# Hybrid GDN/Mamba2 trunk on one core: unit loads on GpSimd's queue, the nested heads' decayed k on VectorE

## Chip, cores and metric

The kernel runs on one core of a Trainium2 chip (TRN2). The metric is the device time of one execution in microseconds (us), and the time of a kernel is the median over its runs. The core's engines have separate instruction queues and work side by side, held together by semaphores: TensorE (PE) for matmuls and transposes into PSUM, VectorE (DVE), ScalarE (ACT), GpSimd (POOL), and SyncE (SP), whose queue here does little but issue DMAs. An engine works through its queue strictly in order, so an instruction that waits holds up all that stand behind it.

## Reference

The reference is one layer (DEPTH = 1) of a macaron trunk over x of 1024 tokens by 1024 channels, in float32: half a SwiGLU, a mixer, half a SwiGLU, a final norm.

```python
x += 1/2 * SwiGLU(RMSNorm(x))                       # D_FF = 2816
h = RMSNorm(x);  p = h @ W_in                       # one combined W_in
x += W_out @ [ GDN_heads(p) || Mamba2_SSD_heads(p) ]   # 8 heads of 128, 16 heads of 64
x += 1/2 * SwiGLU(RMSNorm(x));  out = RMSNorm(x)

def gated_delta_rule(q, k, v, g, beta):             # CHUNK = 64
    q = l2_normalize(q) * dk ** -0.5;  k = l2_normalize(k);  gc = cumsum(g) in a chunk
    a_low = strict_lower(beta * (k @ k.T) * decay)
    t_inv = inverse(eye + a_low)
    u = t_inv @ (v * beta);  w = t_inv @ (k * beta * exp(gc))
    qk = (q @ k.T) * decay;  q_dec = q * exp(gc)
    k_dec = k * exp(gc[-1] - gc)                    # the decayed copy of k
    for each chunk:
        v_new = u - w @ S;  o = q_dec @ S + qk @ v_new
        S = S * exp(g_tot) + k_dec.T @ v_new
```

## The kernel before

**Stages.** The feed-forward parts, the Mamba2 heads and the projection W_in run first and last; in the middle of the program (about 1120 to 1425 us) lie the projections of the last GDN heads, woven into the delta rule of the heads before them. The change touches this middle alone.

**Nested heads.** NESTED is 3 (L654). GDN heads 0 to 2 get their q, k, v and gate z by plain matmuls. Heads 3 to 7, the nested ones, get them by a scheme of seven products in place of eight (Strassen's): the weights of a pair of 128-column blocks have been combined earlier into seven units, each a high and a low part of 128x512 float32 (512 KB), and lie in scratch memory as `wu_scr`. `chunk()` (L1266 to L1290) makes one pair in the order 1, 6, 2, 5, 7, 3, 4; two chunks for each of five heads make 70 units. Each unit is `unit_prod` (L1255): twelve matmuls of 128x512 (L1261 high by high, L1262 high by low, L1263 low by high) into a `pj` bank of PSUM, which ACT copies (L1275, L1280) or DVE adds up (L1271) into `pre`, `zc` and the like. A unit lies in one of four slots of SBUF, tile `wunits`; when the matmuls of unit s have been written, `unit_load(s + 4)` (L1247, its DMA L1252) issues the load of the unit that takes its slot. So a load waits for the last matmul on its slot, and has three units' time until its own first matmul.

**One head of the delta rule.** The causal convolution of q, k and v is an ACT scaling (L1294) and three taps on DVE (L847), with a Silu on ACT (L1419 for v, L1418 for z). `k_part(h)` (L1338): eight PE transposes of k (L1347), four into each of two `mx` banks; for each of the eight blocks, `jd`, a Square on ACT whose accumulator is the token's sum of squares (L1351), and `kd`, the block times `wend`, the decayed copy of k (L1356 on ACT; for the last head, 7, L1353 on DVE). `decays(h)` (L1362) loads the decays (L1366), takes ACT Exps (L1367, L1370) and masks on GpSimd (an affine select, L971). Then kk and qk: L1445 and L1446 write into the `mx` banks, so the first of them waits until `jd` and `kd` have read the bank; DVE makes `u` and `dt` of them (L1449, L1452).

**The inverse.** `u`'s diagonal blocks are stored (L1461) and read back (`fu`, L1488), `fx` is cleared on GpSimd (L1492, L1494), and a solve of 31 steps runs on DVE (L1498, L1500). Its result goes through DMA (L1503, L1510, L1511) and a DVE transpose (L1512). Then PE and the others alternate: L1518/L1519 on PE, L1521 two copies on DVE, L1525 to L1527 on PE, a memset of `x64` on GpSimd (L1529), copies of ACT and DVE (L1530 to L1534), L1539 on PE, L1541 on ACT, L1544 on PE. ACT's L1470 squares q for the head. The recurrence over chunks (L1556 to L1578) uses `kd` at L1570.

**What sets the order.** A tile framework's scheduler puts the instructions of each engine in order, from the dependencies and its own costs. Where a helper's instructions stand in the queue is therefore read from the order, not from the source. Two more loads of 1024 KB on GpSimd's queue, `y` (L1235) and `x` (L1234), fetch the first operands of the output projection (`group_tile`, L1212, matmuls L123 to L125), which begins when the units end, at about 1424.6 us.

Of the kernel before, what the change touches and what calls it, by code (L numbers as in the profile page):

```python
# [11 lines left out]
F32 = mybir.dt.float32  # L12
# [17 lines left out]
GH = 8  # L30
# [14 lines left out]
def kernel(  # L45
# [6 lines left out]
    nc = tc.nc  # L52
    V, A, G, T = nc.vector, nc.scalar, nc.gpsimd, nc.tensor
# [9 lines left out]
    def psum(tag):  # L63
        return ps.tile([P, 512], F32, name="ps_" + tag, tag=tag, bufs=PS_BUFS[tag])
# [9 lines left out]
    wu_scr = [dram.tile([P, 7, 2, 512], F32, name=f"wu_scr{i}") for i in range(2 * (GH - 3))]  # L74
# [579 lines left out]
    NESTED, UP_CHUNKS = 3, 8  # L654
# [592 lines left out]
    def unit_load(s):  # L1247

        if s < 7 * len(wu_scr):
            c, i = divmod(s, 7)  # L1250
            u = slots[s % 4]
            nc.sync.dma_start(out=u.bitcast(F32), in_=wu_scr[c][:, i])  # L1252
            units.append((s, u))

    def unit_prod(bank, m, first):  # L1255

        s, u = units.pop(0)
        bh, bl = H_IN[m]
        for k in range(4):
            wh, wl = (u[:, i, k * P:(k + 1) * P] for i in range(2))  # L1260
            T.matmul(bank, lhsT=wh, rhs=bh[k], start=first and k == 0, stop=False, skip_group_check=True)  # L1261
            T.matmul(bank, lhsT=wh, rhs=bl[k], start=False, stop=False, skip_group_check=True)  # L1262
            T.matmul(bank, lhsT=wl, rhs=bh[k], start=False, stop=k == 3, skip_group_check=True)  # L1263
        unit_load(s + 4)
# [48 lines left out]
    def first_units():  # L1313

        for i in range(2):
            t = wp.tile([P, 2, 2, 512], F32R, name="wunits", tag="wst")
            slots.extend(t[:, j] for j in range(2))
        for s in range(4):
            unit_load(s)
# [15 lines left out]
    with ExitStack() as cg:  # L1335
        g1 = cg.enter_context(tc.tile_pool(name="gdn1", bufs=1, reuse_waits="tile"))
        g2 = cg.enter_context(tc.tile_pool(name="gdn2", bufs=2, reuse_waits="tile"))
        def k_part(h, kt):  # L1338

            tk = g2.tile([P, NB], F32, name="tk")  # L1340
            br2 = g2.tile([P, NB], F32, name="br2")
            kd = g1.tile([P, NB, P], F32, name="kd", bufs=2)
            for half in range(2):
                pt = psum("mx")
                for i in range(4):
                    b = half * 4 + i
                    T.transpose(pt[:, i * P:(i + 1) * P], kt[:, b * P:(b + 1) * P], ident)  # L1347
                for i in range(4):
                    b = half * 4 + i
                    jd = g1.tile([P, P], BF16, name="jd")  # L1350
                    A.activation(out=jd, in_=pt[:, i * P:(i + 1) * P], func=AF.Square, accum_out=tk[:, b:b + 1])  # L1351
                    if h == GH - 1:
                        V.tensor_scalar(out=kd[:, b], in0=pt[:, i * P:(i + 1) * P],  # L1353
                                        scalar1=wend[:, b, h:h + 1], scalar2=None, op0=ALU.mult)
                    else:
                        A.mul(out=kd[:, b], in_=pt[:, i * P:(i + 1) * P], mul=wend[:, b, h:h + 1])  # L1356
            V.tensor_scalar(out=tk, in0=tk, scalar1=EPS, scalar2=None, op0=ALU.add)
            V.reciprocal(out=br2, in_=tk)
            V.tensor_tensor(out=br2, in0=br2, in1=beta[:, :, h], op=ALU.mult)
            return tk, br2, kd  # L1360
# [12 lines left out]
        for h in range(GH):  # L1373
# [25 lines left out]
            else:  # L1399
# [12 lines left out]
                if h < GH - 1:  # L1412
                    tk, br2, kd = k_part(h, kt)
                with tc.issue_after(copy.ins):
                    A.activation(out=qt, in_=qt, func=AF.Silu)
                if h < GH - 1:
                    conv_from(pre, 16 + h, vt_)
                    A.activation(out=zc, in_=zc, func=AF.Silu)  # L1418
                    A.activation(out=vt_, in_=vt_, func=AF.Silu)  # L1419
                else:  # L1420
                    out_start()
                    for b in range(FIRST_TILES):
                        for dh in range(2):
                            tile_end = group_tile(0, b, dh, *ready0[0])
                    tk, br2, kd = k_part(h, kt)
                    qe, dt = decays(h)
                    conv_from(pre, 16 + h, vt_)
                    A.activation(out=zc, in_=zc, func=AF.Silu)
                    A.activation(out=vt_, in_=vt_, func=AF.Silu)
            (G if h == GH - 1 else nc.sync).dma_start(out=z_scr[h], in_=zc)  # L1430
            if h < NESTED:
                tk, br2, kd = k_part(h, kt)
# [5 lines left out]
            u = g2.tile([P, NB, P], F32, name="u")  # L1438
# [68 lines left out]
            x64, mt2 = lv2[0:64, 0], lv2[:, 1]  # L1507
# [18 lines left out]
                T.matmul(px[64:96, ls], lhsT=mt[96:128, b], rhs=xd[96:128, b], start=True, stop=True)  # L1526
                T.matmul(px[32:64, ls], lhsT=xd[32:64, b], rhs=mt[32:64, b], start=True, stop=True)  # L1527
            pxv = px[:, 0:256].rearrange("p (b l) -> p b l", b=NB)
            G.memset(x64[0:32, :, 32:64], 0.0)  # L1529
            A.copy(out=x64[0:32, :, 0:32], in_=xtr[0:32])  # L1530
            A.copy(out=x64[32:64, :, 32:64], in_=xtr[32:64])
            A.mul(out=x64[32:64, :, 0:32], in_=pxv[32:64], mul=-1.0)
# [227 lines left out]
```

## Time and profile before

| | before |
|---|---|
| median of 3 runs | 2300.2 us (2300.33, 2298.66, 2300.2) |
| the profiled execution, its own time | 2300.99 us |
| its span | 2299.3 us |
| granted TensorE clock, mean | 0.997 |
| PE busy | 2253.7 us (98%) |
| PEld (weight loads) busy | 1839.1 us (80%) |
| DVE busy | 1764.1 us (77%) |
| ACT busy | 1176.9 us (51%) |
| POOL busy | 53.1 us (2%) |

The span is the time from the first to the last instruction of one profiled execution; 1.7 us of its own time lie around it, and it is 0.8 us above the median. Times in the trace count from the start of the span. `PE a L1 <- DVE b L2: 2.7, 1, 2.7` says that PE stood still at line 1 for 2.7 us in all, once, 2.7 us the longest, until DVE's line 2 had ended. In a timeline, a bracket at the end of a row is the idle time ahead of the instruction and what ended it.

### The profile page before, as it was taken

How to read it: one execution, taken by the hardware profiler on the slowest of the kernel's cores; microseconds unless marked ns; L12 is line 12 of the kernel's file. 1: busy time of each engine (PE TensorE's matmuls, PEld its weight loads, DVE VectorE, ACT ScalarE, POOL GpSimd, SP SyncE). 2: the span in 40 equal slices, each digit the busy share in tenths (PEclk: the TensorE clock that was granted, in tenths of full speed). 3: DMA queues.
4: the chain of work that ended last, by engine and by line, in shares of the span. 5: the costliest groups of instructions: out<-in, count | busy, mean ns of one | idle time of the engine just before them, and what ended most of it. 6: DMA issues, size and time to landing. Idle time of an engine off the chain costs nothing. (4 is left out here: it accounts for less than half of the span.)

```text
span 2299.3 us, 32056 instructions
## 1 busy us (share of the span) xinstructions
PE 2253.7 (98%) x11630; PEld 1839.1 (80%) x11630; DVE 1764.1 (77%) x3253; ACT 1176.9 (51%) x2279; POOL 53.1 (2%) x115
## 2 busy tenths in 40 slices
PE   7999999999999999999999999999999999999998
PEld 5788888888878878888777887788878888888886
DVE  7998999768777887657577777778688776766787
ACT  7444444354367886875555556623543333334344
POOL 0000000000000110100000000000000000000000
PEclk9999999999999999999999999999999999999999
DMA  3466686496654433242555655436123332329446
GB/s 112 142 228 239 229 274 220 170 336 218 202 183 137 133 120 101 74 131 65 184 164 158 184 164 192 140 99 219 65 88 126 99 113 94 117 87 346 145 151 215
DMA packets 268242, 371.64 MB, mean 162 GB/s; under 512 B 61480, under 2 KB 168076, under 8 KB 266292
## 3 DMA queue, kind: packets, MB, share of 16 engines
q1 hardware_dynamic: 267268, 366.88, 49.0%
q0 software_dynamic: 816, 2.72, 0.3%
q8 instruction: 91, 1.49, 0.3%
q14 instruction: 67, 0.55, 0.1%
HBM read 256.68 MB, written 112.86 MB: 161 GB/s over the span
## 5 line engine op out<-in xcount | busy, mean ns | idle before, releaser
L336 PE MATMUL ps_pj<-bh,al 128*128 128x512 f32 x688 | 267.9, 389 | 0.0
L335 PE MATMUL ps_pj<-bl,ah 128*128 128x512 f32 x688 | 267.8, 389 | 0.0
L334 PE MATMUL ps_pj<-bh,ah 128*128 128x512 f32 x688 | 267.5, 390 | 0.0
L123 PE MATMUL ps_pj<-hhi,whi 128*128 128x512 f32 x512 | 203.3, 397 | 0.4 <-ACT gsb L902 0.4
L125 PE MATMUL ps_pj<-hhi,wlo 128*128 128x512 f32 x512 | 203.7, 398 | 0.0
L124 PE MATMUL ps_pj<-hlo,whi 128*128 128x512 f32 x512 | 202.6, 396 | 0.0
L336 PEld LDWEIGHTS ps_pj<-bh,al 128*128 128x128 f32 x688 | 129.1, 188 | 26.8
L335 PEld LDWEIGHTS ps_pj<-bl,ah 128*128 128x128 f32 x688 | 129.2, 188 | 26.7
L334 PEld LDWEIGHTS ps_pj<-bh,ah 128*128 128x128 f32 x688 | 128.9, 188 | 26.6
L317 DVE TENSOR_TENSOR as<-wst 128x512 f32<-128x512 f32 x220 | 144.8, 689 | 2.0 <-DMA wst<-in_ffn_w_up_dram 1.8
L242 DVE TENSOR_TENSOR al<-as,ah 128x512 fp32r<-128x512 f32 x220 | 141.2, 687 | 4.9 <-ACT ah L241 4.3
L241 ACT CAST hid<-hraw 128x1024 fp32r<-128x1024 f32 (+1 forms) x84 | 82.2, 980 | 119.1 <-PE ps_oo L565 48.7
L334 PE MATMUL ps_mx<-bh,ah 128*128 128x512 f32 x352 | 138.6, 396 | 3.8 <-ACT m L343 1.4
L241 ACT CAST ah<-as 128x512 fp32r<-128x512 f32 x220 | 125.6, 618 | 30.3 <-DVE as L317 30.3
L335 PE MATMUL ps_mx<-bl,ah 128*128 128x512 f32 x352 | 138.4, 393 | 0.4 <-DVE bl L242 0.4
L336 PE MATMUL ps_mx<-bh,al 128*128 128x512 f32 x352 | 137.7, 391 | 0.3 <-DVE al L242 0.3
L241 ACT CAST ah<-wst 128x512 fp32r<-128x512 f32 x88 | 54.5, 621 | 155.9 <-PE ps_oo L335 94.4
L242 DVE TENSOR_TENSOR hid<-hraw,hid 128x1024 fp32r<-128x1024 f32 (+1 forms) x84 | 95.2, 1133 | 22.8 <-ACT hid L241 22.5
L123 PEld LDWEIGHTS ps_pj<-hhi,whi 128*128 128x128 f32 x512 | 96.3, 188 | 19.8 <-ACT gsb L902 0.9
L124 PEld LDWEIGHTS ps_pj<-hlo,whi 128*128 128x128 f32 x512 | 96.3, 188 | 19.3 <-issue 0.8
L125 PEld LDWEIGHTS ps_pj<-hhi,wlo 128*128 128x128 f32 x512 | 96.2, 188 | 19.3 <-issue 0.5
L564 PE MATMUL ps_pj<-wd,hid 128*128 128x512 f32 x264 | 103.4, 392 | 1.3 <-DVE wd L242 1.2
(505 smaller groups left out, 5704.6 us busy)
## 6 DMA issues: line engine op xcount, KB each, us to landing
wu_scr<-wunit SPq DMA_DIRECT2D x140, 256.0 KB, 3.5
hraw<-hid_scr SPq DMA_DIRECT2D x70, 512.0 KB, 3.8
wunits<-wu_scr SPq DMA_DIRECT2D x70, 512.0 KB, 4.1
hid_scr<-hs SPq DMA_DIRECT2D x110, 256.0 KB, 3.2
wst<-in_ffn_w_down_dram SPq DMA_DIRECT2D x50, 512.0 KB, 5.0
wst<-in_ffn_w_gate_dram SPq DMA_DIRECT2D x22, 1024.0 KB, 5.5
wst<-in_ffn_w_up_dram SPq DMA_DIRECT2D x22, 1024.0 KB, 8.6
hid_scr<-sg SPq DMA_DIRECT2D x44, 256.0 KB, 2.0
```

Source lines behind the costliest of these rows:

```text
L123: T.matmul(o, lhsT=wh, rhs=mh, start=first, stop=False)
L124: T.matmul(o, lhsT=wh, rhs=ml, start=False, stop=False)
L125: return T.matmul(o, lhsT=wl, rhs=mh, start=False, stop=last)
L241: return (A.copy(out=hi, in_=src), V.tensor_tensor(out=lo, in0=src, in1=hi.bitcast(F32), op=ALU.subtract))
L242: V.tensor_tensor(out=lo, in0=src, in1=hi.bitcast(F32), op=ALU.subtract))
L317: V.tensor_tensor(out=t, in0=v[0], in1=v[1], op=v[2])
L334: T.matmul(bank, lhsT=wh[:, k], rhs=bh[:, k], start=a, stop=False, skip_group_check=True)
L335: T.matmul(bank, lhsT=wh[:, k], rhs=bl[:, k], start=False, stop=False, skip_group_check=True)
L336: T.matmul(bank, lhsT=wl[:, k], rhs=bh[:, k], start=False, stop=z, skip_group_check=True)
L564: T.matmul(bank, lhsT=hh, rhs=wl, start=False, stop=False, skip_group_check=True)
```

## The change

Three lines change.

```diff
     def unit_load(s):
         if s < 7 * len(wu_scr):
             c, i = divmod(s, 7)
             u = slots[s % 4]
-            nc.sync.dma_start(out=u.bitcast(F32), in_=wu_scr[c][:, i])
+            G.dma_start(out=u.bitcast(F32), in_=wu_scr[c][:, i])
             units.append((s, u))
...
                     A.activation(out=jd, in_=pt[:, i * P:(i + 1) * P], func=AF.Square, accum_out=tk[:, b:b + 1])
-                    if h == GH - 1:
+                    if h >= NESTED:
                         V.tensor_scalar(out=kd[:, b], in0=pt[:, i * P:(i + 1) * P],
                                         scalar1=wend[:, b, h:h + 1], scalar2=None, op0=ALU.mult)
                     else:
                         A.mul(out=kd[:, b], in_=pt[:, i * P:(i + 1) * P], mul=wend[:, b, h:h + 1])
...
-            G.memset(x64[0:32, :, 32:64], 0.0)
+            V.memset(x64[0:32, :, 32:64], 0.0)
```

All 70 unit loads go from SP's queue to GpSimd's; the 32 `kd` of heads 3 to 6 go from ACT (L1356) to DVE (L1353); the eight memsets at L1529 go from GpSimd to DVE. No arithmetic is added or left out. The scheduler then orders the queues anew. On GpSimd, the loads stand in the order of the units but for two pairs that are swapped (48/49 and 52/53), between the `fx` memsets and affine selects of the heads; each waits for PE (its slot is free). PE's matmuls are the same, and in the same order up to head 3's `k_part`.

**Head 4.** PE's queue before, from the last transposes of head 4's `kt` to the first L1445 (`ps_mx_11574` and `ps_mx_11591` are the two banks, `ps_mx_11621` the bank of the first kk, `wunits` the slots, `hhi`, `hlo` and `t4`, `t6` the activations' parts; `[waits X]` names whom a row waits for):

```order
L1347 MATMUL ps_mx_11591<-ident_185,kt_11357 128x128 x4
L1261 MATMUL ps_pj_12041<-hhi_5516,wunits_10080 128x512 [waits DMAHW0_49]
L1262 MATMUL ps_pj_12041<-hlo_5520,wunits_10080 128x512
L1263 MATMUL ps_pj_12041<-hhi_5516,wunits_10080 128x512
L1261 MATMUL ps_pj_12041<-hhi_5516,wunits_10080 128x512
L1262 MATMUL ps_pj_12041<-hlo_5520,wunits_10080 128x512
L1263 MATMUL ps_pj_12041<-hhi_5516,wunits_10080 128x512
L1261 MATMUL ps_pj_12041<-hhi_5517,wunits_10080 128x512
L1262 MATMUL ps_pj_12041<-hlo_5521,wunits_10080 128x512
L1263 MATMUL ps_pj_12041<-hhi_5517,wunits_10080 128x512
L1445 MATMUL ps_mx_11621<-kt_11357 128x128 [waits Activation_49]
L1446 MATMUL ps_mx_11621<-qt_11356,kt_11357 128x128
```

PE's queue now, at the same L1445; the rows are the last of 26 unit matmuls that stand behind the transposes:

```order
L1262 MATMUL ps_pj_12056<-t6_10088,wunits_10080 128x512
L1263 MATMUL ps_pj_12056<-t6_10086,wunits_10080 128x512
L1261 MATMUL ps_pj_12041<-hhi_5518,wunits_10081 128x512 [waits DMASW6_49,Activation_49]
L1262 MATMUL ps_pj_12041<-hlo_5522,wunits_10081 128x512
L1445 MATMUL ps_mx_11621<-kt_11357 128x128 [waits DVE_49]
L1446 MATMUL ps_mx_11621<-qt_11356,kt_11357 128x128
```

The first L1445 has moved back on PE from behind 9 unit matmuls to behind 26, and it waits for DVE where it waited for ACT. In head 3 it has moved from behind 8 to behind 24, in head 6 it stands behind 26.

DVE's queue now, at the same place (`kd_11573` is head 4's; L847 are taps of its v, L1498 and L1500 the last steps of head 3's solve):

```order
L1353 TENSOR_SCALAR kd_11573<-ps_mx_11574,wend_5931 128x128 [waits Activation_49]
L1500 TENSOR_TENSOR fx_11029<-fx_11029,ft_11030 128x7x5 [waits DVE_49]
L847 SCALAR_TENSOR_TENSOR vt__11358<-pre_10673,cols_195,vt__11358 128x1024
L1498 TENSOR_TENSOR ft_11030<-fx_11029,fu_11024 128x28 [waits DVE_49]
L1353 TENSOR_SCALAR kd_11573<-ps_mx_11574,wend_5931 128x128 [waits Activation_49]
L1500 TENSOR_TENSOR fx_11029<-fx_11029,ft_11030 128x7x4 [waits DVE_49]
L847 SCALAR_TENSOR_TENSOR vt__11358<-pre_10673,cols_195,vt__11358 128x1024
L1498 TENSOR_TENSOR ft_11030<-fx_11029,fu_11024 128x24 [waits DVE_49]
L1353 TENSOR_SCALAR kd_11573<-ps_mx_11574,wend_5931 128x128 [waits Activation_49]
L1500 TENSOR_TENSOR fx_11029<-fx_11029,ft_11030 128x8x3 [waits DVE_49]
```

Between this third `kd` and the fourth stand five more steps of the solve (L1498, L1500 and so on) and the memset L1529; the second bank's four `kd` follow with one L1271 between. Before, no `kd` stood there, and the three taps stood together behind the solve. On ACT each `jd` of a nested head but the first now waits for DVE, as in head 7 before, so that `jd` and `kd` take turns.

**Head 5.** PE's queue before, in the inverse of head 4 (`lv2_11785` and `u_11620` are its operands; L979 and L1479 belong to the same head):

```order
L1261 MATMUL ps_pj_12738<-t3_8497,wunits_10081 128x512
L979 MATMUL ps_mx_12357<-qsq_12355,ones_193 32x256 [waits PE_49,Activation_49]
L1539 MATMUL ps_sc_11845<-lv2_11785,u_11620 64x64 [waits Activation_49,Pool_49]
L1539 MATMUL ps_sc_11845<-lv2_11785,u_11620 64x64 x7
L979 MATMUL ps_mx_12357<-qsq_12355,ones_193 32x256 x3
L1479 MATMUL ps_mx_12369<-ident_185,vt__12040 128x128 x4
L1262 MATMUL ps_pj_12738<-t3_8499,wunits_10081 128x512
L1263 MATMUL ps_pj_12738<-t3_8497,wunits_10081 128x512
L1544 MATMUL ps_sc_11855<-u_11620,lv2_11785 64x64 [waits DMAHW0_49,DMAHW6_49,DVE_49,Activation_49]
```

PE's queue now, in the same inverse; 36 unit matmuls stand between head 5's transposes and the first L1518, and the first row is the last of L1525 to L1527:

```order
L1527 MATMUL ps_sc_11814<-lv_11784 32x32
L1539 MATMUL ps_sc_11845<-lv2_11785,u_11620 64x64 [waits Activation_49]
L1539 MATMUL ps_sc_11845<-lv2_11785,u_11620 64x64 x7
L1544 MATMUL ps_sc_11855<-u_11620,lv2_11785 64x64 [waits DMAHW1_49,DMAHW7_49,DVE_49,Activation_49]
L1544 MATMUL ps_sc_11855<-u_11620,lv2_11785 64x64 x7
L1445 MATMUL ps_mx_12303<-kt_12039 128x128 [waits DVE_49]
L1446 MATMUL ps_mx_12303<-qt_12038,kt_12039 128x128
```

L1518, L1525, L1539, L1544 and head 5's first L1445 now stand one behind the other on PE with no unit matmul between; before, unit matmuls stood between each two of them, and the L1445 long ahead of them.

ACT's queue now, at the same place (`jd` reads head 5's first bank):

```order
L1351 ACTIVATE jd_12267,tk_12253<-ps_mx_12256 128x128 [waits Activation_49]
L1532 ACTIVATE lv2_11785<-ps_sc_11814 32x8x32 [waits PE_49]
L1470 ACTIVATE qsq_12355<-qt_12038 128x1024 [waits DMAHW2_49]
L1534 ACTIVATE u_11620<-ps_sc_11814 32x8x32 [waits DVE_49]
L1541 COPY lv2_11785<-ps_sc_11845 64x512 [waits PE_49]
L1351 ACTIVATE jd_12270,tk_12253<-ps_mx_12256 128x128 [waits Activation_49]
```

The third and fourth `jd` of head 5 stand on both sides of the inverse's ACT steps; before, the eight pairs of `jd` and `kd` stood on ACT in one piece, ahead of head 5's Silus.

## Prediction

> **What bounds the kernel now.** I read the page first, for the engine that fills the span.
>
> ```profile
> PE 2253.7 (98%) x11630; PEld 1839.1 (80%) x11630; DVE 1764.1 (77%) x3253; ACT 1176.9 (51%) x2279; POOL 53.1 (2%) x115
> ```
>
> PE is busy for 2253.7 of 2299.3 us. No line of the diff adds or removes a matmul, so the change can only act through the times at which PE stands still. Next comes the view by stretches, for the part from the first unit product to the last (columns: us, then busy us and instructions of PE, PEld, DVE, ACT and POOL, the granted clock, DMA share, GB/s), and the waits of PE in it.
>
> ```profile
> 1121.00:1426.00 305.00, 296.64 (x2045) 235.69 (x2045) 212.56 (x678) 175.09 (x497) 13.53 (x36) 0.99 0.59 174
> ```
>
> ```profile
> PE ps_pj L1261 <- DVE pre L1271: 2.7, 1, 2.7
> PE ps_mx L1445 <- ACT kd L1356: 1.6, 1, 1.6
> PE ps_sc L1556 <- DVE sn L1575: 1.3, 1, 1.3
> PE ps_oo L1567 <- ACT vn L1563: 0.9, 2, 0.5
> PE ps_sc L1561 <- DVE rr L1558: 0.6, 1, 0.6
> PE ps_sc L1518 <- DVE lv L1512: 0.2, 1, 0.2
> ```
>
> PE is idle for 305.00 - 296.64 = 8.4 us in the middle of the program, and the waits explain 7.3 of them. Two things follow. A gain from this change can't be much above 7.3 us. And no wait ends with a unit load: no row names L1252 or DMA. DVE, at 212.56 of 305.00 us, is the busier of the helpers; ACT has 175.09.
>
> I then asked for the tile that changes engine, and for its surroundings in head 4, where the 1.6 us wait lies.
>
> ```profile
> L1356 ACT ACTIVATE kd<-ps_mx,wend x56: 349/392/477, 1009.2 to 1368.8; 128x128 f32<-128x128 f32 x56
> L1353 DVE TENSOR_SCALAR kd<-ps_mx,wend x8: 318/350/351, 1438.5 to 1451.0; 128x128 f32<-128x128 f32 x8
> ```
>
> ```profile
> 1246.41 0.25 ACT L1351 ACTIVATE jd<-ps_mx 128x128 bf16<-128x128 f32 x1
> 1246.91 0.26 ACT L1351 ACTIVATE jd<-ps_mx 128x128 bf16<-128x128 f32 x1
> ...
> 1248.15 0.38 ACT L1356 ACTIVATE kd<-ps_mx,wend 128x128 f32<-128x128 f32 x1
> ```
>
> ```profile
> 1243.83 1.04 PE L1347 MATMUL ps_mx<-ident,kt 128*128 128x128 f32 x8
> 1244.63 0.47 PE L1261 MATMUL ps_pj<-hhi,wunits 128*128 128x512 f32 x1
> ...
> 1246.56 0.40 PE L1263 MATMUL ps_pj<-hhi,wunits 128*128 128x512 f32 x1
> 1248.59 0.49 PE L1445 MATMUL ps_mx<-kt 128*128 128x128 f32 x2 [1.64 <-ACT kd L1356]
> ```
>
> A pair of `jd` and `kd` on ACT takes 1246.91 - 1246.41 = 0.50 us, so the first bank is read 2.1 us after its first `jd` (1248.53). PE transposes at 1243.83, does nine unit matmuls (nine from 1244.63 on, eight steps to 1246.56: 0.24 us each) and stands for 1.64 us before L1445.
>
> The trace has one head whose `kd` are on DVE, head 7. Its timeline is the nearest evidence for heads 3 to 6 after the change.
>
> ```profile
> 1437.21 1.03 PE L1347 MATMUL ps_mx<-ident,kt 128*128 128x128 f32 x8
> 1438.12 0.28 ACT L1351 ACTIVATE jd<-ps_mx 128x128 bf16<-128x128 f32 x1
> 1438.51 0.35 DVE L1353 TENSOR_SCALAR kd<-ps_mx,wend 128x128 f32<-128x128 f32 x1 [3.27 <-ACT jd L1351]
> 1443.80 0.32 DVE L1353 TENSOR_SCALAR kd<-ps_mx,wend 128x128 f32<-128x128 f32 x1
> 1446.97 0.28 ACT L1351 ACTIVATE jd<-ps_mx 128x128 bf16<-128x128 f32 x1
> 1447.38 0.35 DVE L1353 TENSOR_SCALAR kd<-ps_mx,wend 128x128 f32<-128x128 f32 x1 [0.78 <-ACT jd L1351]
> ```
>
> The fourth `kd` ends at 1444.12, 6.0 us after the first `jd`, because each waits its turn behind other work on two queues. Without other work a pair takes 0.41 (1446.97 to 1447.38) plus 0.35, some 0.8 us with the way back, and four take 3.2. So the first bank is free 3.2 to 6.0 us after its first `jd` instead of 2.1. DVE idled ahead of two of these `kd`, and what stands behind them on DVE waited too.
>
> **The change part by part.**
>
> *Unit loads on GpSimd's queue.* SP sheds 70 issues, and the small loads of the inverse that stand behind them may go out earlier. GpSimd must issue in time between its masks and memsets. A load is issued when the last matmul on its slot is done and is wanted three units later, 3 x 12 x 0.24 = 8.6 us in a dense stretch. Now they land like this (minimum, median, maximum):
>
> ```profile
> DMA to landing us min/median/max: 3.5/4.1/4.6
> ```
>
> No load of this size on GpSimd's queue is in the trace. These are the nearest rows (KB each, us to landing):
>
> ```profile
> y<-ssm_scr POOLq DMA_DIRECT2D x1, 1024.0 KB, 6.7
> x<-in_w_out_dram POOLq DMA_DIRECT2D x1, 1024.0 KB, 10.4
> z_scr<-zc POOLq DMA_DIRECT2D x1, 512.0 KB, 3.3
> ```
>
> The ends are 3.3 us for a store of the same size and 10.4 us for a load of twice the size, issued behind `y` while that one was under way. I take 5 us, near the loads on SP and below `y` with its double size: it is under 8.6, and the cost is nothing. If that cover is gone, each load at 10.4 costs 1.8 us on its slot (a rival below). The other work on GpSimd adds little to an issue:
>
> ```profile
> L971 POOL TENSOR_SCALAR_AFFINE_SELECT dt<-dt 128x1024 f32<-128x1024 f32 x8 | 12.7, 1593 | 103.3 <-ACT qe L1367 103.3
> L1529 POOL MEMSET lv<- 32x256 f32 x8 | 2.4, 302 | 132.9 <-DVE ft L1498 128.2 <-DMA mix_scr<-vr 4.8
> ```
>
> An affine select holds the queue for 1.6 us, and 5 + 1.6 is still under 8.6; it waits for ACT's Exp L1367, which in the order is due about when the next slot comes free. `x`, which now stands behind the last unit load, is issued later than before, by as much as its slot takes to come free; no wait in the trace hangs on it. Value: 0, between -0.2 (the one wait of the list, at L1518, that hangs on the inverse's small loads) and +31, worked out with the rival.
>
> *The memset on DVE.* Eight times about 0.3 us on DVE (302 ns on GpSimd is the nearest row) where the solve has just ended. It stands ahead of a `kd` in head 4, so I count it there.
>
> *The 32 `kd` on DVE.* ACT sheds 32 x 0.39 = 12.5 us, DVE gains 32 x 0.35 = 11.2; neither lies on the path as such. What lies on it is when the `mx` banks come free.
>
> Head 4, first bank. PE now arrives after 26 unit matmuls: 1244.63 + 26 x 0.24 = 1250.9. The first `jd` began at 1246.41. In DVE's queue between the first and the fourth `kd` lie two taps, nine solve steps and the memset. Their prices:
>
> ```profile
> 1246.54 3.93 DVE L847 SCALAR_TENSOR_TENSOR vt__11358<-pre,cols,vt__11358 128x1024 f32<-128x1024 f32 x3 [1.81 <-ACT vt__11358 L1294]
> ...
> 1408.60 0.20 DVE L1498 TENSOR_TENSOR ft<-fx,fu 128x50 f32<-128x50 f32 x1
> 1408.84 0.21 DVE L1500 TENSOR_TENSOR fx<-fx,ft 128x50 f32<-128x50 f32 x1
> ```
>
> Taps 2 x 1.3 (a third of 3.93), solve steps 9 x 0.2, memset 0.3, four `kd` 4 x 0.35, first hand-off 0.4: 6.5 us, so the bank is free at 1252.9 and PE waits 2.0 us where it now waits 1.6. At head 7's pace (6.0) it is 1.5, with bare pairs (3.2) nothing. So this bank is worth between -1.6 and +0.4; I take 0, its cost at the two likelier paces being -0.1 and +0.4.
>
> Heads 3 and 6, first bank. By head 7 the first `jd` begins 0.9 us after the transposes (1437.21 to 1438.12) and the bank is free 6.0 later, at 6.9. PE arrives after 0.8 for the transposes and 24 or 26 unit matmuls, at 6.6 or 7.0. Cost 0.3 and 0, with 0 and 1.0 as ends (DVE's queue there holds solve steps as well).
>
> Second banks of heads 3, 4 and 6. Four more pairs take 3.2 to 6.0 us, while PE has about 12 unit matmuls and the first kk and qk, about 3.7 us: 0 to 2.3 each. I take 1.0 each, 3.0 together, nearer the bare pairs because in head 4 the four stand almost side by side on DVE.
>
> Head 5. PE runs through L1518, L1525, L1539, L1544 and the first L1445 without a unit matmul between. What each waits for, from head 7's timeline:
>
> ```profile
> 1443.09 1.07 ACT L1470 ACTIVATE qsq<-qt 128x1024 f32<-128x1024 f32 x1
> 1445.34 0.88 DVE L1521 COPY lv<-ps_sc 32x256 f32<-32x256 f32 x2
> 1447.99 0.38 ACT L1532 ACTIVATE lv<-ps_sc 32x256 f32<-32x256 f32 x1 [0.65 <-PE ps_sc L1527]
> 1449.71 0.38 ACT L1534 ACTIVATE u<-ps_sc 32x256 f32<-32x256 f32 x1
> 1450.00 0.56 ACT L1541 COPY lv<-ps_sc 64x512 f32<-64x512 f32 x1
> ```
>
> L1525 waits for the copies, 0.9. L1539 waits for three ACT steps that stand in a row, 0.38 + 1.07 + 0.38 = 1.8. L1544 waits for L1541, 0.6. L1445 waits for the `jd` and `kd` behind that, 0.8 less L1544's own time, some 0.2. Sum 3.5 us. Each of these steps needs what PE made in the step before, so none can be done early except L1470, and 2.4 is the low end; 4.5 the high one, with a quarter of a microsecond for each of the four hand-offs.
>
> *Sum.* 0 + 0 + 0.3 + 0 + 3.0 + 3.5 = 6.8 us, say 7. Of the present waits the 2.7 us at L1261 stay: the L1271 behind it stands on DVE, which gets busier. Taken from the profiled execution's own time, 2300.99, that is 2308; that execution is 0.8 above the median of the runs, 2300.2, so the forecast is 2307.
>
> The price of a `kd` has the trace slightly in DVE's favour, 350 against 392 ns. The Trainium skill, "Perfetto Trace Analysis", section "Optimizing Scalar/DVE Operations", speaks against the change: it gives an overhead of about 125 ns for VectorE and 51 ns for ScalarE on operations that touch PSUM. By it, an estimate, each `kd` would hold DVE 74 ns longer than ACT, four in a row 0.3 us, and four heads 1.2 us more than the sum, 2308. The measured durations don't show it, and I go by them.
>
> **The rivals.** *No change you can measure* (0.2%, 4.6 us, is about what a measurement of this kernel can tell from no change). The L1445 stand 17 matmuls later than before, and if the pairs run at 0.8 us instead of head 7's 1.5, every first bank is ready; head 5 then costs its 2.4, the second banks nothing, and head 4's 1.6 is gone: +0.8, 2301. For it: DVE is free for 92 of the 305 us. Against: head 7's pace, and the inverse of head 5.
>
> *Faster.* ACT freed by 12.5 us and SP by 70 issues let the inverse and the recurrence run earlier, and the waits at L1445, L1556, L1567 and L1561 go: 1.6 + 1.3 + 0.9 + 0.6 = 4.4; with the 2.7 at L1261 gone as well, 7.1, which is the most there is. 2293 to 2296. For it: two of these waits end with ACT. Against: DVE, on which the others hang, gets more work and waits in order for ACT.
>
> *Much slower: unit loads late.* If a load on GpSimd's queue lands after 10.4 us, it is 10.4 - 8.6 = 1.8 us late, once in four units, as four slots go round together. With 70 units that is 17 x 1.8 = 31 us if all stretches were dense; with 305 / 70 = 4.4 us per unit, other matmuls lie between in about half, so 15 us: 2315. It decides from a landing of 8.6 us on. Against: the store of 3.3 us, and that GpSimd's issue of `x` and DVE's solve ran side by side, the two steps at 1408.60 and 1408.84 keeping their 0.2 us within this row:
>
> ```profile
> 1408.29 0.74 POOL L1234 DMA_DIRECT2D x<-in_w_out_dram  x1
> ```
>
> The Trainium skill, "SBUF — State Buffer", the box "The 'DVE blocks DMA' trap" in section "SBUF: two separate sides", has a rule for this rival: the descriptors of a GpSimd load can't be written while DVE runs an operation in a two-port mode. No run here shows it.
>
> **How the numbers follow.** My forecast, slower by 4.6 to 14 us, has 0.47. No change has 0.28, faster 0.18, late loads 0.07. The likeliest time is 2307. Two in ten may lie outside: the lower half of the faster case and the upper part of the late loads, so the range runs from 2295 (5 us of the 7.1 gained) to 2316, just above the late loads' 2315 and the sum of all upper ends: 0.4 + 1.0 + 1.0 + 3 x 2.3 + 4.5 = 14 us, 2314. Slower is 0.47 + 0.07 = 0.54, same 0.28, faster 0.18.
>
> **What would show it.** Right: unit loads on GpSimd's queue landing below 8 us and no PE wait on them; in the waits of PE, L1445 behind DVE's `kd` several times, about 3 to 5 us in all; around 1310 to 1325 us, L1525, L1539 and L1544 waiting, together about 3 us. Wrong: `kd` pairs at 0.8 us and no L1445 in the list (no change or faster); a unit's first L1261 waiting for L1252 (late loads); a clock other than 0.99 in the middle.

## The result, and the profile after

The changed kernel takes 2316.6 us (median of 4 runs, 2313.0 to 2318.7), the kernel before in the same comparison 2300.3 (4 runs, 2298.7 to 2301.5): a ratio of 1.0073, 95% interval 1.0057 to 1.0088. It is slower by 16.4 us. The forecast was 2307, slower by 7, with 2316 as the upper end.

The page of the changed kernel answers to the first line that the prediction shows:

```profile
span 2316.9 us, 32054 instructions
...
PE 2262.1 (98%) x11630; PEld 1847.7 (80%) x11630; DVE 1775.1 (77%) x3293; ACT 1174.3 (51%) x2249; POOL 88.7 (4%) x177
```

The span grew by 2316.9 - 2299.3 = 17.6 us. PE has the same 11630 instructions, and still its busy time grew from 2253.7 to 2262.1, by 8.4 us. The other 9.2 us are idle time (2316.9 - 2262.1 = 54.8 against 45.6). These are figures of one profiled execution, which took 2318.7 us. So two things happened: PE stood still for longer, and the same matmuls took longer. The prediction has only the first of them.

The stretch of the unit products, and PE's waits in it and behind it (us in total, times, longest):

```profile
1121.00:1426.00 305.00, 292.07 (x2006) 235.04 (x2005) 215.86 (x680) 163.82 (x446) 45.70 (x98) 0.98 0.60 171
```

```profile
PE ps_sc L1518 <- DVE lv L1512: 5.9, 4, 4.6
PE ps_pj L1261 <- DVE pre L1271: 2.6, 1, 2.6
PE ps_mx L1445 <- DVE kd L1353: 2.5, 2, 1.3
PE ps_sc L1544 <- ACT lv L1541: 0.7, 1, 0.7
PE ps_sc L1525 <- DVE lv L1521: 0.5, 1, 0.5
PE ps_sc L1539 <- ACT lv L1532: 0.5, 1, 0.5
```

```profile
PE ps_mx L1445 <- DVE kd L1353: 4.8, 2, 4.0
```

The last fence is the part behind 1440 us, where this row wasn't there before. The waits name two places, and the view in stretches of 10 us shows that at both the granted clock (the third number from the end) fell:

```profile
1310.00:1320.00 10.00, 4.75 (x49) 3.55 (x48) 1.74 (x6) 8.79 (x19) 1.87 (x3) 0.87 0.86 234
1320.00:1330.00 10.00, 8.84 (x92) 8.11 (x93) 3.60 (x8) 4.39 (x14) 0.00 (x0) 0.50 0.01 3
1450.00:1460.00 10.00, 5.25 (x33) 4.12 (x33) 6.55 (x13) 9.57 (x28) 0.40 (x1) 0.87 0.30 56
1460.00:1470.00 10.00, 10.00 (x120) 7.72 (x116) 5.84 (x17) 4.02 (x9) 0.00 (x0) 0.62 0.50 183
```

In the kernel before, the first and the third of these rows are:

```profile
1310.00:1320.00 10.00, 10.00 (x85) 8.30 (x83) 5.73 (x23) 5.39 (x8) 0.00 (x0) 1.00 0.74 184
1450.00:1460.00 10.00, 10.00 (x80) 8.31 (x80) 8.05 (x26) 5.52 (x15) 0.00 (x0) 1.00 0.17 49
```

PE was busy throughout at a clock of 1.00. Now it is idle for 5.25 and 4.75 us of the first and the third, and runs at 0.50 and 0.62 in those behind them.

The first place is head 5's `k_part` beside head 4's inverse. ScalarE and VectorE there:

```profile
1308.48 0.26 ACT L1351 ACTIVATE jd<-ps_mx 128x128 bf16<-128x128 f32 x1
...
1308.84 1.28 ACT L1418 ACT_TABLE_LOAD   x1
1310.13 1.06 ACT L1418 ACTIVATE zc<-zc 128x1024 f32<-128x1024 f32 x1
1311.21 1.28 ACT L1370 ACT_TABLE_LOAD   x1
1312.51 2.45 ACT L1370 ACTIVATE dt<-dt,ngc 128x128 f32<-128x128 f32 x8
1314.86 0.25 ACT L1351 ACTIVATE jd<-ps_mx 128x128 bf16<-128x128 f32 x1
```

```profile
1315.24 0.35 DVE L1353 TENSOR_SCALAR kd<-ps_mx,wend 128x128 f32<-128x128 f32 x1 [5.15 <-ACT jd L1351]
1317.47 0.45 DVE L1512 STREAM_TRANSPOSE lv<-lv 128x256 f32<-128x256 f32 x1 [1.88 <-DMA lv<-fs_x]
```

From the first `jd` of the bank to the second it takes 6.4 us: a Silu, eight Exps and two table loads stand between them. The second `kd` waits for the second `jd`, and PE's order has head 5's kk and qk behind head 4's whole inverse. So nothing is left for PE to do while the inverse's operands come back from memory: it stands before L1518 for 4.6 us (VectorE's L1512 had to wait for that load, not for the `kd`), and then before each step:

```profile
1317.97 0.26 PE L1518 MATMUL ps_sc<-lv,u 32*32 32x32 f32 x1 [4.59 <-DVE lv L1512]
...
1321.56 1.97 PE L1539 MATMUL ps_sc<-lv,u 64*64 64x64 f32 x16 [0.47 <-ACT lv L1532]
1324.19 1.96 PE L1544 MATMUL ps_sc<-u,lv 64*64 64x64 f32 x16 [0.67 <-ACT lv L1541]
```

The second place is head 7, whose lines the diff doesn't touch. Its second bank's products now stand right behind the first bank's:

```profile
1452.66 0.49 PE L1445 MATMUL ps_mx<-kt 128*128 128x128 f32 x2 [0.77 <-DVE kd L1353]
1453.20 0.39 PE L1445 MATMUL ps_mx<-kt 128*128 128x128 f32 x2
1457.80 0.79 PE L1445 MATMUL ps_mx<-kt 128*128 128x128 f32 x2 [3.98 <-DVE kd L1353]
```

The first of these matmuls, right behind a wait of 0.77 us, takes 0.49 us; the third, right behind the wait of 3.98 us, takes 0.79.

### The profile page after: what moved, and what is told of

The parts are those of the page before. It is cut to its first block, busy times and chain, and to the rows that moved or that the text cites. A ratio compares the mean times of both kernels' runs of the same rounds, so it can differ in the third digit from the quotient of the medians.

```text
span 2316.9 us, 32054 instructions
## 1 busy us (share of the span) xinstructions
PE 2262.1 (98%) x11630; PEld 1847.7 (80%) x11630; DVE 1775.1 (77%) x3293; ACT 1174.3 (51%) x2249; POOL 88.7 (4%) x177
## 3 DMA queue, kind: packets, MB, share of 16 engines
q1 hardware_dynamic: 257188, 330.18, 43.4%
## 4 chain that ended last, share of the span: by engine, by line
PE 64%; DVE 18%; ACT 7%; DMA 6%; issue 4%; SPq 1%; POOL 0%; DVEq 0%; ACTq 0%; POOLq 0%
PE ps_pj L125 6%; PE ps_pj L123 6%; PE ps_pj L124 6%; PE ps_pj L334 4%; PE ps_pj L335 4%; PE ps_pj L336 4%; PE ps_mx L334 2%; PE ps_mx L336 2%; PE ps_mx L335 2%; DVE al L242 2%; DMA wst<-in_ffn_w_down_dram 2%; PE ps_pj L564 1%; PE ps_pj L565 1%; PE ps_pj L563 1%; DVE ft L1498 1%
## 5 line engine op out<-in xcount | busy, mean ns | idle before, releaser
L123 PE MATMUL ps_pj<-hhi,whi 128*128 128x512 f32 x512 | 203.3, 397 | 0.4 <-ACT gsb L902 0.4
L123 PEld LDWEIGHTS ps_pj<-hhi,whi 128*128 128x128 f32 x512 | 96.3, 188 | 19.7 <-ACT gsb L902 0.8
```

What stands on the lines that cost most here:

```text
L123: T.matmul(o, lhsT=wh, rhs=mh, start=first, stop=False)
```

## Experiments

Several explanations were held against each other. "Turns" (later "hand-off"): ScalarE and VectorE taking turns over `jd` and `kd` costs, wherever it stands. "Loads": GpSimd's queue costs. "Engines": an operation costs more on its new engine. "Order": neither engine nor queue costs anything by itself, but each edit makes the scheduler write another order, and some orders leave PE without work at two or three places. Beside "order" stands "clock" (the halved clock behind a gap costs as much as the gap) against "waiting only".

### Each edit alone, and in pairs

The six kernels have one or two of the diff's three edits. L1353 on VectorE alone:

```diff
-                    if h == GH - 1:
+                    if h >= NESTED:
```

> Only the kd of heads 3 to 6 move to VectorE; unit loads stay on SP's queue and the memset on GpSimd. Theory 'order' (the time was lost at two places where the scheduler's new order leaves PE nothing to do, head 4's inverse with no large matmul between its steps and head 7's second bank right behind its first, and each stall of over 4 us is followed by about 10 us at half clock): here head 4's inverse has 3, 2 and 2 large matmuls between its steps, but head 7's second L1445 stands right behind the first bank's, so only the second place costs: 2306 to 2310, with a dip of the granted clock near 1450 us and none near 1315 us. Theory 'turns' (kd on VectorE costs by itself, since jd and kd take turns, wherever PE's instructions stand): the whole loss, 2314 to 2318. Theory 'loads' (unit loads on GpSimd's queue cost): 2299 to 2302.

The unit loads alone:

```diff
-            nc.sync.dma_start(out=u.bitcast(F32), in_=wu_scr[c][:, i])
+            G.dma_start(out=u.bitcast(F32), in_=wu_scr[c][:, i])
```

> Only the 70 unit loads move to GpSimd's queue. Theory 'order': the order changes here too, but every head's first L1445 stands 8 unit matmuls behind its transposes as before, and no inverse lacks matmuls throughout (two have none between the first two steps): 2299 to 2305, no stall over 3 us but the old one of 2.7. Theory 'turns': no change, 2299 to 2302. Theory 'loads': 2310 to 2318, with waits of PE on the unit loads or loads that land after 7 us.

The first edit with the memset of L1529 (`G.memset` to `V.memset`), loads on SP:

> The kd and the memset move to VectorE; the unit loads stay on SP's queue. Theory 'order': head 4's inverse has 2, 2 and 1 large matmuls between its steps and head 7's second bank 18 matmuls behind the first, so neither place stalls as in the changed kernel: 2301 to 2306, no stall over 4 us in the middle. Theory 'turns': 2314 to 2318. Theory 'loads': 2299 to 2302.

The first two edits, memset on GpSimd:

> The kd move to VectorE and the unit loads to GpSimd's queue; the memset stays on GpSimd. Theory 'order': head 4's inverse has 0, 2 and 2 large matmuls between its steps, head 5's 0, 1 and 4, head 7's second bank stands 10 behind the first; some stalls of 1 to 3 us, 2302 to 2309. Theory 'turns': 2314 to 2318. Theory 'loads': 2310 to 2318.

Loads and memset, `kd` on ScalarE; PE's order is that of the loads alone, instruction by instruction:

> Unit loads on GpSimd's queue and the memset on VectorE; the kd of heads 3 to 6 stay on ScalarE. PE's queue is word for word that of the kernel with the loads alone (2314). Theory 'order': that kernel's time, 2308 to 2318, with the same three stalls at L1518. Theory 'engines': the memset on VectorE takes one wait from GpSimd's queue, which the loads then pass sooner: 2299 to 2306.

The memset alone; PE's order is that of the kernel before:

> Only line 1529's memset on VectorE, the other two edits undone; TensorE's order is that of the kernel before, instruction by instruction. Theory 'order': the same time as before within 0.15%, 2298 to 2304 us, with the granted clock at 0.997. Rival 'engines' (an instruction more on VectorE in the inverse's chain costs by itself, 0.3 us a head): 2303 to 2306 us.

Measured. Span, PE's busy time and the rest of the span are those of the profiled execution:

| edits | median us | ratio to before | span | PE busy | rest |
|---|---|---|---|---|---|
| none | 2301 | 1 | 2299.3 | 2253.7 | 45.6 |
| memset | 2299.2 | 0.9983 [0.9975, 0.9992] | 2300.0 | 2256.6 | 43.4 |
| kd | 2318.1 | 1.0078 [1.0060, 1.0097] | 2312.7 | 2259.2 | 53.5 |
| loads | 2314.2 | 1.0051 [1.0034, 1.0067] | 2316.4 | 2269.1 | 47.3 |
| kd, memset | 2297.4 | 0.9983 [0.9974, 0.9992] | 2297.6 | 2252.6 | 45.0 |
| kd, loads | 2301.1 | 0.9998 [0.9988, 1.0009] | 2300.2 | 2252.8 | 47.4 |
| loads, memset | 2316.9 | 1.0064 [1.0047, 1.0082] | 2315.9 | 2268.1 | 47.8 |
| all three | 2316.6 | 1.0073 [1.0057, 1.0088] | 2316.9 | 2262.1 | 54.8 |

The first row is the kernel before, with its median in the comparisons with the six (2301.3 to 2301.6); each ratio is to the kernel before of the same comparison.

`kd` alone costs 17 us and the loads alone 13, but both together cost nothing. No fixed price per edit gives that. (`kd` with the memset, and the memset alone, come out 0.17% faster than before; both intervals end just below 1, and no run here says what gave the 2 to 4 us.) "Turns" as a price that is paid everywhere falls with the two pairs that have all the `kd` on VectorE and cost nothing, "loads" as such a price with the pair that has the loads and costs nothing, "engines" with both and with the memset alone. What agrees is the order: the two kernels with one PE order (loads; loads and memset) have one time, and the memset with the order of before stays within 0.2% of before.

But four of the six times lay outside what "order" expected. `kd` alone was to take 2306 to 2310 us and took 2318, the loads alone 2299 to 2305 and took 2314; the times of both are those that "turns" and "loads" had named. The two pairs with `kd` came out 4 us and 1 us below their ranges. So the orders, as they were read before the runs, didn't give the places: with `kd` alone PE waits for 6.30 us at head 5's L1445, where no gap was expected, for 3.41 us at L123 and for 2.93 us at head 7's L1445.

In the kernel with the loads alone PE waits at three places, at line 1518:

```profile
PE ps_sc L1518 <- DVE lv L1512: 7.6, 3, 2.7
```

```profile
1310.00:1320.00 10.00, 7.25 (x70) 6.21 (x69) 5.95 (x20) 5.70 (x15) 0.53 (x1) 0.86 0.54 156
1320.00:1330.00 10.00, 10.00 (x88) 5.96 (x87) 2.30 (x11) 2.73 (x8) 0.00 (x0) 0.50 0.10 15
1380.00:1390.00 10.00, 7.50 (x79) 5.96 (x80) 5.56 (x22) 4.58 (x8) 0.53 (x1) 0.78 0.46 129
1390.00:1400.00 10.00, 10.00 (x95) 6.69 (x86) 1.77 (x9) 2.85 (x8) 0.00 (x0) 0.50 0.09 14
```

The 7.6 us of waiting replaced waits that the kernel before had, so the rest of the span grew by only 1.7 us (47.3 - 45.6); PE's busy time grew by 15.4. Nearly the whole loss of that profiled execution is clock.

These three waits also say that the loads have something like a price on one path. Each ends with L1512, which itself waited 2.4, 3.2 and 2.8 us for the inverse's loads (L1510). From the first store (L1503) to L1512 that round trip through memory took 13.7 to 14.4 us there. In the kernel before, L1512 waited for these loads in one head, and the trip took 11.4 us:

```profile
1305.00 2.55 SPq L1503 DMA_DIRECT2D fs_x<-fx  x4
```

```profile
1316.37 0.45 DVE L1512 STREAM_TRANSPOSE lv<-lv 128x256 f32<-128x256 f32 x1 [0.60 <-DMA lv<-fs_x]
```

Whether GpSimd's queue or the new order on SP's makes the trip longer, no run here separates. In the pair of `kd` and loads PE pays little for it: 1.4 us in all at L1518.

### Cover for head 7's second bank

The two kernels of this part differ from each other only in the matmuls that PE does between the two banks; some products are made several times over with the same result, nothing is left out.

```diff
-                for i in range(2):
+                for i in [0, 1] * (2 if h == GH - 1 and b0 == 0 else 1):
```

> The changed kernel, with head 7's first kk/qk pair of blocks computed twice: four extra matmuls of 128x128, whose results are the same, stand in the 4 us in which PE waits for the second bank. It is the twin of the next kernel, which repeats them three times more; all engines have the same order in both but for those twelve matmuls. Theory 'clock' (half of the loss is the halved clock that follows PE's idle time, and not the idle time): the wait of 3 us that is left is followed by a dip as in the changed kernel, 2312 to 2318. Theory 'waiting' (only the idle time itself counts): 2312 to 2318 as well.

The same line with 5 in place of 2:

> The same with head 7's first kk/qk blocks computed five times: sixteen extra matmuls, 3.6 us, fill the wait for the second bank, and end no later than it does. Theory 'clock': no dip of the granted clock near 1455 to 1470 us, and 3 to 6 us less than the twin with four extra matmuls, though it does 2.7 us more work. Theory 'waiting': the same time as the twin, or up to 1 us more.

Measured: 2314.6 us (1.0055 [1.0042, 1.0068]) with the small cover, 2311.2 (1.0045 [1.0033, 1.0057]) with the large one, the ranges overlapping (2310.4 to 2316.1, 2310.6 to 2313.6). At the place itself the profiles are clear. The small cover:

```profile
1458.80 0.80 PE L1445 MATMUL ps_mx<-kt 128*128 128x128 f32 x2 [3.09 <-DVE kd L1353]
```

```profile
1450.00:1460.00 10.00, 6.14 (x34) 5.05 (x33) 6.33 (x13) 9.16 (x29) 1.40 (x1) 0.93 0.21 33
1460.00:1470.00 10.00, 10.00 (x133) 7.93 (x132) 7.59 (x23) 6.33 (x11) 0.00 (x0) 0.90 0.57 206
```

The large one, at the same matmul and in the stretches around it:

```profile
1454.80 0.49 PE L1445 MATMUL ps_mx<-kt 128*128 128x128 f32 x2 [0.41 <-DVE kd L1353]
```

```profile
1450.00:1460.00 10.00, 9.54 (x117) 7.89 (x118) 8.50 (x20) 8.93 (x20) 0.00 (x0) 1.00 0.52 150
1460.00:1470.00 10.00, 9.91 (x120) 8.06 (x110) 7.05 (x22) 4.95 (x9) 0.42 (x2) 1.00 0.36 99
```

The gap is filled, and the clock stays at 1.00 behind it, where the twin has 0.93 and 0.90. "Waiting only" has no reason for that, and none for a gain, since work that replaces a wait one for one gains nothing; "clock" has. How much time it gains isn't settled: the 3.4 us of medians come from runs that overlap, and of the 3.5 us between the two profiled spans (2312.8 and 2309.3) the clock at this place explains 1.7 (20 us less 18.3 at 0.93 and 0.90). The rest lies elsewhere, above all at the first place (1310 to 1340 us), where the half clock cost 6.8 us in the one profile and 5.1 in the other.

### Two edges in the scheduler's order

The first edge holds head 4's L1518 behind the unit that the kernel before has there (unit 46), so that unit matmuls lie between the steps of the inverse (`held` is an empty dict at the start, `prod` the last matmul of the unit, L1263):

```diff
-        unit_load(s + 4)
+        unit_load(s + 4); [tc.add_manual_dep(held[h].ins, prod.ins.name, mybir.DependencyInfo(mybir.DependencyClass.NoSync, mybir.DependencyReason.DATA), reason='held') for h, w in ((4, 46),) if w == s]
...
-                T.matmul(pm[32:64, ls], lhsT=u[0:32, b, 32:64], rhs=xtr[0:32, b], start=True, stop=True)
+                held.setdefault(h, T.matmul(pm[32:64, ls], lhsT=u[0:32, b, 32:64], rhs=xtr[0:32, b], start=True, stop=True))
```

> The changed kernel with all three of its lines, and one edge for the scheduler that orders the issue and waits for nothing: the first L1518 of head 4's inverse is queued behind one more unit (unit 46). The scheduler then puts 5, 4 and 5 large matmuls between the steps of that inverse, and 46 and 64 ahead of head 7's first two banks. Theory 'order': no stall over 3 us, a mean clock of 0.996 to 0.998, 2296 to 2304. Theory 'engines' (the three assignments cost by themselves, together): 2312 to 2319.

Measured: 2318.4 us, 1.0069 [1.0057, 1.0082]. This expectation failed. The wait at L1518 is gone, and one twice as long stands at head 5's first product:

```profile
1320.38 0.79 PE L1445 MATMUL ps_mx<-kt 128*128 128x128 f32 x2 [9.53 <-DVE kd L1353]
```

ScalarE's order hadn't changed: the Exps still stood between head 5's first `jd` and the later ones. With the `kd` edit alone the same wait is 6.30 us at the same place. Counting PE's matmuls between two steps was not enough; the chain of the other engines has to be read to its end. So the second edge goes there. It puts the Exps of line 1370 of heads 5 and 6 behind the last `jd` of the same head (`last` is the result of line 1351):

```diff
-            V.tensor_scalar(out=tk, in0=tk, scalar1=EPS, scalar2=None, op0=ALU.add)
+            [tc.add_manual_dep(e.ins, last.ins.name, mybir.DependencyInfo(mybir.DependencyClass.NoSync, mybir.DependencyReason.DATA), reason='held') for e in exps.get(h, ()) if h in (5, 6)]; V.tensor_scalar(out=tk, in0=tk, scalar1=EPS, scalar2=None, op0=ALU.add)
...
-                A.activation(out=dt[:, b], in_=dt[:, b], func=AF.Exp, bias=ngc[:, b, h:h + 1])
+                exps.setdefault(h, []).append(A.activation(out=dt[:, b], in_=dt[:, b], func=AF.Exp, bias=ngc[:, b, h:h + 1]))
```

> All three lines of the change stay; a scheduling edge that costs no semaphore puts ScalarE's Exps of line 1370 (the decay tables of heads 5 and 6) behind the last Square of line 1351 of the same head, so that in head 5 the eight Exps no longer stand between the first Square and the second. In the order that follows, the three steps of head 4's inverse have 3, 2 and 4 groups of large matmuls between them (0, 0 and 0 in the changed kernel), and head 7's second bank stands 18 groups behind its first (0 in the changed kernel). Theory 'order' (the 16 us are TensorE's gaps at two places, the halved clock behind them included, and neither the engines nor the queue): no wait over 2.3 us between 1250 and 1470 us, granted clock 0.996 to 0.998, 2296 to 2304 us. Rival 'hand-off' (the decayed copies on VectorE have to wait for their turn there whatever the order, and the loads on GpSimd's queue add to that): waits of 4 us and more remain at line 1445, 2310 to 2318 us.

And the same for head 5 alone:

> The same edge for head 5 alone. Head 5's Squares are in one row and head 4's inverse has 3, 2 and 4 groups of large matmuls between its steps, but head 5's own inverse now has none before its second and third step, and head 7's second bank 12 groups behind its first. Theory 'order': the 4.6 us wait near 1313 us is gone; one of 1 to 3 us may come up at head 5's inverse near 1380 us, with or without a halved clock behind it: 2299 to 2310 us, above the kernel with the edge for both heads. Rival 'hand-off': as there, 2310 to 2318 us, the two alike.

Measured: 2305.2 us for both heads (12 runs, 2299.0 to 2308.9; 1.0011 [1.0000, 1.0022]) and 2309.1 for head 5 alone (12 runs, 2300.1 to 2315.0; 1.0028 [1.0016, 1.0040]), within the 2299 to 2310 that "order" gave. With all three edits of the change in place, the edge for both leaves 3.9 us of the loss (2305.2 against 2301.3 for the kernel before in the same comparison), where the changed kernel loses 16.4. In its profile head 5's products come ahead of head 4's L1518 and shorten the wait there from 4.59 to 1.29 us:

```profile
1313.34 0.44 PE L1445 MATMUL ps_mx<-kt 128*128 128x128 f32 x2
...
1316.67 0.21 PE L1518 MATMUL ps_sc<-lv,u 32*32 32x32 f32 x1 [1.29 <-DVE lv L1512]
```

No wait over 2.3 us is left, as "order" expected, and "hand-off" with its 4 us and 2310 to 2318 us is out. But the time is 1 us above the expected 2304, and the clock not at 0.996 in each run:

```profile
1320.00:1330.00 10.00, 10.00 (x72) 8.63 (x66) 3.96 (x17) 4.44 (x11) 0.46 (x1) 0.50 0.31 107
```

The clock fell to half even behind the 1.29 us. Of the 12 runs of this one program the four with a mean clock of 0.998 took 2299.0 to 2300.9 us, the three with 0.994 took 2308.1 to 2308.9. The runs of the kernel before at 0.998, in the same comparison, took 2299.1 to 2301.0. At the same clock, then, the changed kernel with this edge is as fast as the kernel before; the rest of its loss is clock.

## Why the prediction was right and wrong

The sign and the mechanism that it forecast were right in part: waits behind DVE's `kd` and a bare inverse of head 4. Idle time grew by 9.2 us where it summed 6.8. But the terms that make up the two sums are not the same, so that 6.8 stands near 9.2 by luck, and a second loss of 8.4 us, the clock, was put at nothing without a reason. By its steps:

- **Unit loads: cost 0.** Right for the loads themselves. They land in a median of 4.3 us instead of the estimated 5:

```profile
DMA to landing us min/median/max: 3.7/4.3/6.9
```

  All are below the 8.6 us of cover, and no wait of PE ends with one. The Trainium skill's trap, "SBUF — State Buffer", section "SBUF: two separate sides", the box "The 'DVE blocks DMA' trap", didn't show: VectorE was busy for 215.86 of the 305 us, and the slowest of 70 loads took 6.9. Whether VectorE's operations ran in the port mode that the rule speaks of, the trace doesn't say.

  Wrong for what it said of the inverse's small loads, that they may go out earlier when SP sheds 70 issues. In head 4's inverse the trip from L1503 to L1512 took 14.0 us (from this row to 1317.47) where it had taken 11.4:

```profile
1303.52 2.61 SPq L1503 DMA_DIRECT2D fs_x<-fx  x4
```

  By an estimate from these two figures, 2.6 of the 4.6 us before L1518 come from that.

- **The price of a kd and of the memset: nothing.** Right: 345 ns a `kd` on VectorE (350 expected), and the memset alone on VectorE leaves 0.9983 of the time.
- **First banks of heads 3, 4 and 6: 0.3 us.** Close: the list has 2.5 us at L1445 in two waits, and the kernel before had 1.6 there, so 0.9 more.
- **Second banks of heads 3, 4 and 6: 3.0 us.** Wrong: none of them waited.
- **Head 5: 3.5 us.** The place was right, the terms not. L1525, L1539 and L1544 waited 0.5, 0.5 and 0.7 (0.9, 1.8 and 0.6 forecast), and L1445 not at all. The largest wait, 4.6 us, was at L1518 itself. The prediction listed PE's steps from L1518 on and priced what each waits for, except the first: it didn't ask when L1518's operands are back from memory, now that PE has 36 unit matmuls and nothing else ahead of it.
- **Head 7: not considered.** It isn't in the diff, its `kd` were on VectorE before. But the edit moved PE's order there too, and it lost 4.8 us at L1445 where it had lost no time. The 3 us that the sum put on the second banks of other heads stood in its place by chance.
- **The clock: not priced.** With the wait at L1518 and head 7, this is the step that failed, and the largest part of it. The sum took it that PE's matmuls cost what they cost before, so that the change could act only through the times at which PE stands still, and counted each wait at its own length. Behind the two long ones PE ran at half clock for another 10 us and more, and its busy time grew by 8.4 us with the same 11630 instructions. The prediction named "a clock other than 0.99 in the middle" as a sign against it, and that row says 0.98.
- **The rivals.** Late loads would have given the measured time (2315) by another way, and the profile rules it out. "No change" and "faster" fell with head 5.

A deeper fault lies under these. The sum added up prices edit by edit. The table of the eight kernels shows that this program has no such prices: what an edit costs depends on the order that the scheduler makes of it. The same three edits took 2317 us in one order and 2305 in another, and 2299 to 2301 in those runs of it in which the clock held.

## What to carry to other kernels

Before pricing an edit of a scheduled kernel, compare the orders of all engines over the whole program, also where the diff changes nothing, and look on PE for steps that have lost the work between them; then follow the chain that each waits for through the helper engines and the memory to its end. Price a gap on PE as its length plus half the length of the stretch at low clock that may follow it: here that doubled the loss. The first line of a profile's page tells the two apart: idle time grows with waits, and busy time with an unchanged count of instructions grows with a lower clock.

## What the runs showed of the hardware

The clock halves behind short gaps. A wait of 2.5 us in the kernel with the loads alone was followed by 0.50 for the stretch from 1390 to 1400 us, and one of 1.29 us in the kernel with the second edge by 0.50 from 1320 to 1330. It doesn't do so each time: the wait of some 2.6 us at L1261 comes with a clock of 0.83 from 1170 to 1180 us in the kernel before and of 1.00 in the changed one.

The traces show why. In all thirteen, each stretch at half clock but those at the program's two ends lasts a whole number of times 3.41 us: 13.65 and 10.24 us (four and three times) at the two places of the changed kernel, 17.07 us (five times) twice in the kernel with the loads alone. Cut into windows of this length, in step with these stretches, the kernel before has its wait at L1261 in one window, and half clock in the next (columns as in the rows of 10 us; the ends of matmuls are modelled):

```profile
1170.00:1173.41 3.41, 0.86 (x4) 0.38 (x2) 3.41 (x8) 1.82 (x2) 0.00 (x0) 1.00 0.70 219
1173.41:1176.83 3.42, 3.32 (x8) 2.65 (x9) 3.41 (x8) 1.17 (x3) 0.00 (x0) 0.50 0.23 91
```

In the changed kernel the windows happen to cut that wait in two, and the clock stays at 1.00:

```profile
1170.73:1174.14 3.41, 2.48 (x11) 1.71 (x10) 3.41 (x7) 0.21 (x1) 1.05 (x2) 1.00 0.34 103
1174.14:1177.55 3.41, 1.70 (x7) 1.43 (x8) 3.41 (x7) 2.72 (x3) 0.01 (x1) 1.00 0.80 292
```

So it goes in all these traces where a window at full clock has large matmuls alone (those that use all of the array): half clock followed each one in which PE was busy for 1.52 us or less, and none in which it was busy for 1.8 or more; between the two it went both ways. The inverse's small matmuls (32 and 64 columns) count for less than their time. Behind the wait of 1.29 us PE was busy for 2.12 us of the window, 34 of the 39 matmuls were small, and half clock followed; a window of the kernel before with 2.11 us of large matmuls (1207.55 to 1210.96) had none behind it:

```profile
1315.23:1318.64 3.41, 2.12 (x39) 1.49 (x39) 1.85 (x6) 1.93 (x5) 0.00 (x0) 1.00 0.31 123
1318.64:1322.06 3.42, 3.42 (x56) 2.50 (x56) 2.27 (x10) 2.11 (x5) 1.05 (x2) 0.50 0.42 111
```

The same holds for the way back. A window of large matmuls alone that kept PE busy for 2.9 us or more ended the half clock each time; the second row above, busy throughout but mostly with small matmuls, didn't. That fits the 10 us and more of half clock at the places above, all beside an inverse, and the one window of it behind the wait at L1261.

One program's runs differ by it: in the 12 runs with the second edge, 0.001 of mean clock went with 2.1 us (a straight line through them), close to the 2.3 us that 0.001 of 2300 us is. The Trainium skill, "TensorE: Matmul & The Clock Gate", "Part 1: The HAM clock gate", has a half rate after an idle window of about 3.4 us, in windows that run freely. The half rate and the length of the windows agree, and windows that start anywhere fit results that differ between runs. That the window has to be idle doesn't agree: 1.52 us of large matmuls in it, or 2.12 us of mostly small ones, were not enough to keep the clock.
